# Attention on one core: pair 1 copied in two halves from two PSUM banks, and another set of VectorE groups

## Chip, cores and metric

The kernel runs on one core of a Trainium2 chip. The metric is device time in microseconds (us): the median of five runs. Times inside an execution come from the hardware profile of one run and count from its first instruction. The engines are TensorE (PE, with its weight loads as PEld), VectorE (DVE), ScalarE (ACT), GpSimd (POOL) and SyncE (SP), which issues most DMAs.

## The reference

Plain softmax attention for 8 x 8 = 64 heads, 512 queries and keys of 64 numbers each, fp32 in and out:

```python
batch, heads, seq, dim = 8, 8, 512, 64
scale = 1.0 / np.sqrt(q.shape[-1])
scores = np.einsum('bhqd,bhkd->bhqk', q, k) * scale
scores = scores - scores.max(axis=-1, keepdims=True)
attn = np.exp(scores)
attn = attn / attn.sum(axis=-1, keepdims=True)
return np.einsum('bhqk,bhkd->bhqd', attn, v).astype(np.float32)
```

## The kernel before

**Tiling.** The 64 heads are 32 pairs g of two heads h. For every head the 512 keys are four chunks c of 128. One block (g, c, h) is a score tile of 128 keys by 512 queries. Two blocks make a group m; there are 129 groups, the last two with one block each. Pair 0 has groups 0 to 3, pair 1 groups 4 to 7, and so on.

**The path of a pair.** The loads bring q, k, v in fp32 (`load`, L311). `cast` (L323) makes fp16 copies on GpSimd: q and k into `qkp`, v into `vp`, which also has a column of ones, so that the sum of the weights comes out of the value product. Only q of pair 1 is cast on VectorE. `transposes` (L377) runs four TensorE transposes for the keys and, at its second call, four for the queries, all into one PSUM tile `tp`. `copy` (L386) moves it to `tqk` in SBUF. `scores` (L398) multiplies a block of keys by the queries into a PSUM tile `st`, of which there are three; group m uses the one that group m - 3 used. ScalarE then takes the exponential of the group (L421) into `pt`.

**Eight groups on VectorE.** For the groups in `ON_DVE`, VectorE computes the exponential instead: `raise_` (L433) reads `st` into integers and frees it, and five passes (L448) finish it into `pd`. The passes can be done at any later time between other VectorE work.

**Values and output.** `values` (L495) is one unit of four matmuls into an `o` tile: 128 queries of one head. Seven units share a tile; the count of units begins at 4, so that the first tile holds three. `normalise` (L476) multiplies by the reciprocal of the sums into `ring`, from where the output is stored head by head.

**The two shared banks.** The tiles `tp` and `o` alternate in two PSUM banks, x0 and x1. A bank comes free when VectorE has copied or normalised what is in it.

**The order.** Every engine works through its instructions in program order, and that order is written by a planner, the class `Plan` (L17). It steps through time with assumed costs in nanoseconds (L31 to L38) and lets TensorE (`step_pe`, L168) and VectorE (`step_dve`, L191) choose their next piece of work. TensorE takes the next scores if their `st` tile is free and either the next group's is too, or the work that ScalarE has ahead of it (the backlog) is under `HURRY`, or the last thing was scores as well. If the tile is not free yet, but will be within `SOON` while the backlog is under `BACKLOG`, TensorE waits. Otherwise it takes transposes or value units. VectorE takes what is ready, a raise first; with nothing ready it starts a pass, unless a known copy would be late by more than `LATE_COPY` or a norm or raise by more than `LATE_NORM` at its end. A group is on VectorE by the list alone:

```python
    ON_DVE = (6, 15, 32, 44, 58, 69, 90, 103)

    LATE_NORM, LATE_COPY, HURRY, SOON, BACKLOG = 1000, 1400, 1000, 80, 1000
```

**Casts.** `feed(g)` (L364) is called with the first group of each pair. It loads pair g + 6 and casts later pairs; from pair 3 on the casts are held and given to GpSimd one at a time, each tied to the VectorE work before it (`release`, L348). `FIRST_VALUES` (L278) says which v is cast when in the first pairs. The first pair has its own opening, `first_pair` (L555), which leaves x0 and x1 to `tp_kb` and `tp_qb`; the planner takes over at group 3.

Of the kernel before, what the change touches and what calls it, by code (L numbers as in the profile page):

```python
# [9 lines left out]
FP16 = mybir.dt.float16  # L10
# [6 lines left out]
class Plan:  # L17
# [16 lines left out]
    TO_ACT, TO_DVE, TO_PE = 275, 210, 60  # L34

    COPY, NORM, RAISE = (615, 700), (307, 390), (1145, 1225)
    NORM_COLUMN, PASS_DONE = 67, 80
    PASSES = (650, 1230, 1230, 1230, 1230)  # L38
    FIRST_EXP = 5260
    STEP = 5  # L40
    FIRST_UNIT = 4
    ON_DVE = (6, 15, 32, 44, 58, 69, 90, 103)

    LATE_NORM, LATE_COPY, HURRY, SOON, BACKLOG = 1000, 1400, 1000, 80, 1000
    MARGIN, SLACK = 1.05, 0

    def __init__(self, groups, pairs, first):
# [37 lines left out]
    def for_dve(self, m):  # L85
        return m in self.ON_DVE

# [103 lines left out]
    def step_dve(self, t):  # L191
        now = [x for x in self.ready if x[0] <= t]
        if now:
            job = min(now, key=lambda x: (x[1] != "raise", x[0]))
            self.ready.remove(job)
            _, kind, what = job
            self.note(t, kind, *what)
            if kind == "norm":
                more = self.NORM_COLUMN * what[1]
                self.dve = t + self.NORM[0] + more  # L200
                self.banks[what[2]] = t + self.NORM[1] + more + self.TO_PE
            elif kind == "copy":
                self.dve = t + self.COPY[0]
                self.banks[what[1]] = self.tq[what[0]] = t + self.COPY[1] + self.TO_PE
            else:
                self.dve = t + self.RAISE[0]
                self.read[what[0]] = t + self.RAISE[1] + self.TO_PE
                self.passes += [(what[0], s) for s in range(len(self.PASSES))]
        elif self.passes:
            m, s = self.passes[0]  # L210
            end = t + int(self.MARGIN * self.PASSES[s])
            late = {"copy": self.LATE_COPY, "norm": self.LATE_NORM, "raise": self.LATE_NORM}
            if all(x[0] > end - late[x[1]] for x in self.ready):
                self.passes.pop(0)
                self.note(t, "pass", m, s)
                self.dve = end
                if s == len(self.PASSES) - 1:
                    self.exps[m] = end + self.PASS_DONE + self.TO_PE + self.SLACK
# [15 lines left out]
def kernel(  # L234
# [7 lines left out]
    nc = tc.nc  # L242
    B, H, S, D = q.shape
    P = 128
    NI = S // P
# [26 lines left out]
    ps_x = ctx.enter_context(tc.tile_pool(name="ps_x", bufs=1, space=bass.MemoryType.PSUM))  # L272
# [2 lines left out]

    HALVED = range(20, 25)
    AHEAD_FROM = 3
    FIRST_VALUES = {0: (), 1: (2,), 2: (1,), 3: (4,), 4: (5, 3), 5: (6, 7), 6: (8, 9)}  # L278
    NU = 56
    ring = cpool.tile([P, NU, D], FP32, name="ring")  # L280
    vps = [cpool.tile([P, 2, NI, D + 1], FP16, name=f"vp{n}") for n in range(NV)]
# [5 lines left out]
    tqk = {}  # L287
    tps = {}
# [51 lines left out]
    held = []  # L340
# [3 lines left out]
    def dve(ins):  # L344
        latest[:] = [ins]
        return ins

    def release(n=1):  # L348
        for g, name in held[:n]:
            ins = cast(g, name)  # L350
            if latest:
                tc.add_manual_dep(ins.ins, latest[0].ins.name, SYNC, reason="SBUF ports")
        del held[:n]

    def hold(g, names):
        held.extend((g, name) for name in names if g < NP)
        while len(held) > 6:
            cast(*held.pop(0))

    def needed(g, names):  # L360
        while any((g, name) in held for name in names):
            cast(*held.pop(0))

    def feed(g):  # L364
# [4 lines left out]
        if g >= AHEAD_FROM:  # L369
            hold(g + 4, "kq")  # L370
        for n in FIRST_VALUES.get(g, (g + 3,)):
            if g < AHEAD_FROM:
# [4 lines left out]
    def transposes(g, n, bank):  # L377
        if n == 0:
            needed(g, "kq")
            tqk[g] = tpool.tile([P, 2, S], FP16, tag="tqk", name=f"tqk_{g}")  # L380
            tps[g] = ps_x.tile([P, 2, NI, P], FP16, tag=f"x{bank}", name=f"tp_{g}")
        n = 1 - n
        for i in range(NI):
            nc.tensor.transpose(tps[g][:, n, i, :], qkp[g][:, n, i, :], ident)  # L384

    def copy(g):  # L386
        if g == 1:
            for n in (1, 0):
                dve(nc.vector.tensor_copy(out=tqk[g][:, n], in_=tps[g][:, n].rearrange("p i c -> p (i c)")))
            return  # L390
        release()
        dve(
            nc.vector.tensor_copy(  # L393
                out=tqk[g][:, :, :], in_=tps.pop(g).rearrange("p n i c -> p n (i c)")
            )
        )
# [247 lines left out]
    with tc.manual_schedule():  # L644
# [15 lines left out]
        for g, names in ((1, "kq"), (0, "v"), (2, "kq")):  # L660
            for name in names:
                cast(g, name)
        feed(0)
        do = {
            "transposes": transposes,
            "scores": scores,
            "values": values,
            "feed": feed,
            "raise": raise_,
            "copy": lambda g, b: copy(g),  # L670
            "pass": pass_,
            "norm": lambda u, n, b: normalise(u, n),
# [33 lines left out]
```

## Time and profile before

| | |
|---|---|
| five runs | 121.69, 122.01, 121.75, 122.77, 122.33 us; median 122.01 |
| the profiled execution | 122.12 us, of it a span of 120.3 us from first to last instruction |
| granted TensorE clock | 0.999 |
| busy in the span | ACT 112.6 us (94%), DVE 105.5 (88%), PE 103.0 (86%), POOL 66.6 (55%) |
| HBM traffic | read 25.17 MB, written 8.39 MB |
| exponentials on ScalarE (L421) | 118, 107.7 us busy |
| last exponential | ends at 116.5 us |

In the lines of a timeline the columns are start, length, engine, line of the program, operation, what is written and read, how often, and in brackets how long the engine stood idle before and which instruction ended that. Lines that merge several instructions give the time from the first start to the last end. Overlapping instructions of one engine, such as exponentials of which the next starts before the last has ended, count once in busy times.

### The profile page before, as it was taken

The numbers are of one execution on the slowest core, as the hardware profiler recorded it, in microseconds if no ns is written. First come the engines' busy times: TensorE is split into PE (matmuls) and PEld (weight loads), VectorE is DVE, ScalarE is ACT, GpSimd is POOL, SyncE is SP. The second block draws the span as 40 slices with busy tenths as digits, with TensorE's granted clock in tenths as the row PEclk, the third lists the DMA queues.
The fourth block names the chain that finished last, engine by engine and source line by source line (L and its number), as shares of the span: only waits on it lengthen the run. The fifth ranks groups of instructions, "written<-read, shape, count | busy, mean of one in ns | idle before, by whom it ended". The sixth has DMA issues, their size and how long they took to land.

```text
span 120.3 us, 4001 instructions
## 1 busy us (share of the span) xinstructions
PE 103.0 (86%) x1557; PEld 65.6 (55%) x1557; DVE 105.5 (88%) x177; ACT 112.6 (94%) x125; POOL 66.6 (55%) x101
## 2 busy tenths in 40 slices
PE   7969696988899789989897879999988989799970
PEld 2534353664656545845464548666655667367550
DVE  1549999999999999998999999999999999986261
ACT  4689998999999999999999999999999999999970
POOL 2358967999995656344958433596355654210000
PEclk9999999999999999999999999999999999999999
DMA  3999999999999999999999998999999812224243
GB/s 111 270 351 382 381 380 384 383 380 358 326 327 340 311 300 295 312 298 362 335 348 297 312 315 292 310 368 313 332 341 335 285 48 96 87 91 140 93 157 105
DMA packets 35604, 33.83 MB, mean 281 GB/s; under 512 B 2688, under 2 KB 35584, under 8 KB 35584
## 3 DMA queue, kind: packets, MB, share of 16 engines
q1 hardware_dynamic: 35152, 33.24, 83.9%
q10 hardware_dynamic: 432, 0.33, 0.9%
q8 instruction: 12, 0.20, 0.7%
q14 instruction: 8, 0.07, 0.2%
HBM read 25.17 MB, written 8.39 MB: 279 GB/s over the span
## 4 chain that ended last, share of the span: by engine, by line
DVE 29%; ACT 22%; DMA 17%; PE 17%; issue 8%; SPq 3%; POOL 1%; ACTq 0%; POOLq 0%
ACT pt L421 22%; DVE y L466 8%; PE st L416 8%; PE o L505 7%; DMA q<-in_q_dram 6%; DVE ring L482 6%; DVE tqk L393 5%; DMA out_dram<-ring 4%; DMA v<-in_v_dram 4%; DVE pd L466 3%; DVE z L438 3%; DVE m L454 2%; DMA k<-in_k_dram 2%; SPq L321 2%; PE tp L384 2%
## 5 line engine op out<-in xcount | busy, mean ns | idle before, releaser
L421 ACT ACTIVATE pt<-st 128x1024 f16<-128x1024 f32 (+1 forms) x118 | 107.7, 1204 | 1.2 <-PE st L416 1.2
L416 PE MATMUL st<-tqk 64*128 64x512 f16 x248 | 44.4, 382 | 6.6 <-ACT pt L421 5.3
L505 PE MATMUL o<-vp,pt 128*128 128x65 f16 x944 | 42.5, 194 | 2.7 <-DVE tqk L393 1.0
L505 PEld LDWEIGHTS <-pt 128*128 128x128 f16 x944 | 36.2, 98 | 14.7 <-issue 11.9
L333 POOL CAST qkp<-k 128x512 f16<-128x512 f32 x31 | 19.1, 615 | 23.7 <-PE st L416 5.6
L327 POOL CAST vp<-v 128x512 f16<-128x512 f32 x32 | 26.6, 836 | 4.9 <-DVE y L466 2.4
L333 POOL CAST qkp<-q 128x512 f16<-128x512 f32 x30 | 21.7, 725 | 7.7 <-DVE y L466 2.3
L482 DVE TENSOR_TENSOR ring<-o,rc 128x448 f32<-128x448 f32 (+2 forms) x37 | 22.6, 612 | 1.3
L416 PEld LDWEIGHTS <-tqk 64*128 64x128 f16 x248 | 12.2, 93 | 19.8 <-issue 13.1
L384 PE MATMUL tp<-ident,qkp 128*128 128x128 f16 x248 | 19.4, 220 | 3.1 <-DVE tqk L393 1.3
L466 DVE SCALAR_TENSOR_TENSOR y<-y,m 128x1024 f32<-128x1024 f32 x16 | 21.6, 1352 | 0.1
L384 PEld LDWEIGHTS <-qkp 128*128 128x128 f16 x248 | 14.3, 97 | 11.8 <-POOL qkp L333 5.6
L393 DVE COPY tqk<-tp 128x1024 f16<-128x1024 f16 x30 | 20.5, 682 | 0.0
L466 DVE SCALAR_TENSOR_TENSOR y<-m 128x1024 f32<-128x1024 uint32 x8 | 11.2, 1402 | 0.1
L480 DVE RECIPROCAL rc<-o 128x7 f32<-128x7 f32 (+2 forms) x37 | 7.2, 195 | 4.2 <-PE o L505 4.0
L438 DVE TENSOR_SCALAR z<-st 128x1024 uint32<-128x1024 f32 x8 | 9.7, 1217 | 0.7 <-PE st L416 0.7
L466 DVE SCALAR_TENSOR_TENSOR pd<-y,z 128x1024 uint32<-128x1024 f32 x8 | 10.3, 1283 | 0.0
L505 PE MATMUL o<-vp,pd 128*128 128x65 f16 x64 | 9.3, 194 | 0.0
L505 PEld LDWEIGHTS <-pd 128*128 128x128 f16 x64 | 6.3, 98 | 0.7 <-issue 0.5
L454 DVE TENSOR_SCALAR m<-z 128x1024 uint32<-128x1024 uint32 x8 | 6.3, 783 | 0.0
L553 PE MATMUL st_0a<-const-bfloat16-1.0 128*128 128x512 bf16 (+1 forms) x11 | 3.3, 457 | 0.8 <-PEq L690 0.8
L569 ACT ACT_TABLE_LOAD x1 | 1.3, 1283 | 1.7 <-PEq L690 1.7
(44 smaller groups left out, 18.8 us busy)
## 6 DMA issues: line engine op xcount, KB each, us to landing
out_dram<-ring SPq DMA_DIRECT2D x63, 128.0 KB, 3.9
k<-in_k_dram SPq DMA_DIRECT2D x31, 256.0 KB, 4.9
q<-in_q_dram SPq DMA_DIRECT2D x31, 256.0 KB, 5.0
v<-in_v_dram SPq DMA_DIRECT2D x27, 256.0 KB, 5.4
v<-in_v_dram SPq DMA_DIRECT2D x10, 128.0 KB, 3.8
k<-in_k_dram ACTq DMA_DIRECT2D x2, 128.0 KB, 2.7
q<-in_q_dram SPq DMA_DIRECT2D x2, 128.0 KB, 2.5
out_dram<-obl SPq DMA_DIRECT2D x1, 64.0 KB, 1.6
```

Of the source, the lines that this page charges most:

```text
L327: return nc.gpsimd.tensor_copy(out=vps[g % NV][:, :, :, 0:D], in_=raw[g]["v"][:, :, :, :])
L333: return eng.tensor_copy(out=qkp[g][:, "qk".index(name)].rearrange("p i (h d) -> p h i d", h=2), in_=raw[g][name][:, :, :, :],)
L384: nc.tensor.transpose(tps[g][:, n, i, :], qkp[g][:, n, i, :], ident)
L393: nc.vector.tensor_copy(out=tqk[g][:, :, :], in_=tps.pop(g).rearrange("p n i c -> p n (i c)"))
L416: nc.tensor.matmul(st[:, x, :], kc, qc, start=True, stop=True)
L421: nc.scalar.activation(out=pt[:, 0:size, :], in_=st[:, 0:size, :], func=EXP, scale=scale)
L438: nc.vector.tensor_scalar(out=r["z"][:, :, :], in0=r["st"][:, :, :], scalar1=scale * 1.4426950408889634 * 2.0**26, scalar2=15 * 2.0**26, o ...
L454: nc.vector.tensor_scalar(out=r["m"][:, :, :], in0=r["z"][:, :, :], scalar1=0x03FFFFFF, scalar2=0x04000000, op0=AluOp.bitwise_and, op1=Alu ...
L466: nc.vector.scalar_tensor_tensor(out=r["bits"][:, :, :] if n == 3 else r["y"][:, :, :], in0=r["m"][:, :, :] if n == 0 else r["y"][:, :, :] ...
L480: nc.vector.reciprocal(out=rc[:, 0:n], in_=o[:, x : x + n, D : D + 1])
L482: nc.vector.tensor_tensor(out=ring[:, u % NU : u % NU + n, :], in0=o[:, x : x + n, 0:D], in1=rc[:, 0:n].broadcast_to([P, n, D]), op=AluOp. ...
L505: nc.tensor.matmul(os[u // 7][:, u % 7, :], blocks[(g, c, h)][:, y * P : (y + 1) * P], vps[g % NV][:, h, c, :], start=(c == 0), stop=(c == ...
```

## The change

Three things are edited. First, pair 1: its keys and its queries are transposed into two PSUM tiles, the keys in the planner's bank and the queries in the other one (`bank ^ n`), and the copy of the keys is issued directly behind the keys' transposes; the planner's `copy` step then copies the queries alone. Second, the planner assumes other costs for that step, `COPY_1`. Third, the list of VectorE groups, four of the planner's limits and the order in which v of pairs 3 to 6 is cast are replaced.

```diff
     COPY, NORM, RAISE = (615, 700), (307, 390), (1145, 1225)
+    COPY_1 = (400, 490)
...
-    ON_DVE = (6, 15, 32, 44, 58, 69, 90, 103)
-
-    LATE_NORM, LATE_COPY, HURRY, SOON, BACKLOG = 1000, 1400, 1000, 80, 1000
+    ON_DVE = (6, 16, 34, 49, 61, 74, 87, 98)
+
+    LATE_NORM, LATE_COPY, HURRY, SOON, BACKLOG = 1300, 1400, 900, 220, 1600
...
             elif kind == "copy":
-                self.dve = t + self.COPY[0]
-                self.banks[what[1]] = self.tq[what[0]] = t + self.COPY[1] + self.TO_PE
+                held, done = self.COPY if what[0] != 1 else self.COPY_1
+                self.dve = t + held
+                self.banks[what[1]] = self.tq[what[0]] = t + done + self.TO_PE
...
-    FIRST_VALUES = {0: (), 1: (2,), 2: (1,), 3: (4,), 4: (5, 3), 5: (6, 7), 6: (8, 9)}
+    FIRST_VALUES = {0: (), 1: (2,), 2: (1,), 3: (3,), 4: (5, 6), 5: (4, 7), 6: (8, 9)}
...
             needed(g, "kq")
             tqk[g] = tpool.tile([P, 2, S], FP16, tag="tqk", name=f"tqk_{g}")
-            tps[g] = ps_x.tile([P, 2, NI, P], FP16, tag=f"x{bank}", name=f"tp_{g}")
+        if n == 0 or g == 1:
+
+            tps[g] = ps_x.tile([P, 2, NI, P], FP16, tag=f"x{bank ^ n}", name=f"tp_{g}_{n}")
         n = 1 - n
         for i in range(NI):
             nc.tensor.transpose(tps[g][:, n, i, :], qkp[g][:, n, i, :], ident)
-
-    def copy(g):
+        if g == 1 and n == 1:
+            copy(g, n)
+
+    def copy(g, n=0):
         if g == 1:
-            for n in (1, 0):
-                dve(nc.vector.tensor_copy(out=tqk[g][:, n], in_=tps[g][:, n].rearrange("p i c -> p (i c)")))
+            dve(
+                nc.vector.tensor_copy(
+                    out=tqk[g][:, n], in_=tps[g][:, n].rearrange("p i c -> p (i c)")
+                )
+            )
             return
```

## The prediction

> **What bounds the kernel now.** I read the page's busy shares first, then the windows by stage, then the timeline of ScalarE alone, then the timeline of every engine around pair 1 and of VectorE behind it. The windows show engine by engine how much of each stretch is filled.
>
> ```profile
> core 0: us, PE busy (x) PEld busy (x) DVE busy (x) ACT busy (x) POOL busy (x), PEclk, DMA share, GB/s
> 9.30:20.00 10.70, 8.19 (x110) 4.79 (x107) 10.44 (x13) 10.19 (x11) 8.69 (x11) 1.00 1.09 381
> ...
> 33.00:62.00 29.00, 26.24 (x408) 16.85 (x406) 28.18 (x44) 29.00 (x33) 17.96 (x29) 1.00 1.00 323
> 62.00:100.00 38.00, 34.30 (x542) 22.53 (x541) 37.38 (x56) 38.00 (x43) 20.93 (x34) 1.00 0.90 294
> ```
>
> From 33 to 100 us ScalarE (ACT) has work in every microsecond: 29.00 of 29.00, 38.00 of 38.00. VectorE is nearly as full (28.18, 37.38), but only its lateness can hurt, through what TensorE waits for. So the time is the run of exponentials plus the holes in it. ScalarE's own timeline shows the holes:
>
> ```profile
> 9.31 10.19 ACT L421 ACTIVATE pt<-st 128x1024 f16<-128x1024 f32 x11 [0.64 <-PE st L416]
> 20.04 96.50 ACT L421 ACTIVATE pt<-st 128x1024 f16<-128x1024 f32 x106 [0.54 <-PE st L416]
> ```
>
> Start, length, count; idle before in brackets. One exponential behind a hole takes 1.02 us; the ten others of the first stretch add (10.19 - 1.02) / 10 = 0.917 each. So each hole costs its idle plus 1.02 - 0.917 = 0.11 of lost overlap: 0.75 at the first group of pair 1 (m = 4) and 0.65 at m = 17. In the long stretch the last two half groups take 0.98, which leaves (96.50 - 0.98 - 1.02) / 103 = 0.9175, hence some 0.07 lost in 96 us. **All that can be won in the stream is 0.75 + 0.65 + 0.07 = 1.47 us.** The change keeps eight groups on VectorE, so the number of exponentials stays, and the 120.3 - 116.5 = 3.8 us behind the last exponential is untouched by its lines.
>
> **Pair 1's copies.** The timeline of all engines there:
>
> ```profile
> 7.02 0.43 DVE L333 CAST qkp<-q 128x512 f16<-128x512 f32 x1 [0.81 <-DMA q<-in_q_dram]
> ...
> 7.09 0.81 PE L384 MATMUL tp<-ident,qkp 128*128 128x128 f16 x8 [0.21 <-POOL qkp L333]
> 7.50 0.23 PEld L384 LDWEIGHTS <-qkp 128*128 128x128 f16 x4 [0.18 <-DVE qkp L333]
> ...
> 7.73 0.62 POOL L327 CAST vp<-v 128x512 f16<-128x512 f32 x1 [0.69 <-DMA v<-in_v_dram]
> 7.93 0.76 DVE L389 COPY tqk<-tp 128x512 f16<-128x512 f16 x2 [0.49 <-PE tp L384]
> 8.40 0.54 PE L505 MATMUL o<-vp,pt 128*128 128x65 f16 x12 [0.50 <-POOL vp L327]
> ...
> 8.87 0.82 PE L416 MATMUL st<-tqk 64*128 64x512 f16 x6
> ```
>
> The keys' four transposes are over before the queries' begin at 7.50, yet the keys' copy waits until 7.93, when all eight have ended. With the queries in the other bank it starts at about 7.52 and lasts 0.42 (the mean of these two); VectorE is free from 7.45. The queries' copy starts at 7.93 and ends at 8.36 instead of 8.69. Two copies, eight transposes, no DMA: no count changes. Bank x1, which the queries' tile now takes, was last read by the copy of tp_qb at 5.59 (0.42 long), so nothing waits for it. The first o tile takes the same bank and must now wait for the queries' copy, 8.36; its matmuls wait for the V cast until 8.35 anyway. That cover is 0.01 thin, and each ns past it would delay the first scores by as much.
>
> But what went ahead of the first scores at 8.87 was the twelve value matmuls, not the copy. Here the planner decides. I followed its rules by hand over pair 1 to 4 (its clock, in ns, is used for order alone). Before, the pair is due at 8745 and three value units go at 8300, 8430, 8560. Now it is due at 7985 + 490 + 60 = 8535; after one unit, at 8430, that is less than SOON = 220 off, so TensorE waits. Four matmuls instead of twelve: eight at a pitch of (0.54 - 0.19) / 11 = 0.032 are 0.25 us, so the scores start at 8.62 and the exponential at 9.05: **-0.25**. The bounds are nothing (V comes later) and -0.46 (scores right behind the copy, at 8.41).
>
> **What the new order does to VectorE behind it.** The two units left over hold bank x1; their normalisation moves behind raise 6 and copy 2. The planner puts scores 6 at 9885 instead of 9280 (the slot comes free 39 ns after the planner looks, with a backlog of 1885, over BACKLOG; a value unit, the transposes of pair 2 and another unit go first). So raise 6, the norm and the first two passes all precede copy 3. VectorE's timeline has the durations:
>
> ```profile
> 8.98 0.18 DVE L480 RECIPROCAL rc<-o 128x3 f32<-128x3 f32 x1 [0.29 <-PE o L505]
> 9.20 0.36 DVE L482 TENSOR_TENSOR ring<-o,rc 128x192 f32<-128x192 f32 x1
> 9.74 1.23 DVE L438 TENSOR_SCALAR z<-st 128x1024 uint32<-128x1024 f32 x1 [0.19 <-PE st L416]
> 10.88 0.68 DVE L393 COPY tqk<-tp 128x1024 f16<-128x1024 f16 x1
> 11.48 0.91 DVE L454 TENSOR_SCALAR m<-z 128x1024 uint32<-128x1024 uint32 x1
> 12.42 1.51 DVE L466 SCALAR_TENSOR_TENSOR y<-m 128x1024 f32<-128x1024 uint32 x1
> 13.85 0.68 DVE L393 COPY tqk<-tp 128x1024 f16<-128x1024 f16 x1
> ```
>
> Copy 2 can start at 10.2 (POOL's query cast for pair 2, on TensorE's path, ends at 9.14 + 0.62; four transposes 0.4), so raise 6 at 10.8. By starts: raise 1.14, norm 0.55, first pass 0.94, second 1.43, then the copy's 0.68: copy 3 ends at 15.54 instead of 14.53. Scores 12 take 0.39 and two hand-overs of 0.05: exponential 12 at 16.03. ScalarE would be ready earlier: from 9.05 seven exponentials (4, 5, 7 to 11) at 0.917 make the eighth end at 9.05 + 1.02 + 6.42 = 16.49, against 16.03 + 1.02 = 17.05. A **new hole of about 0.55**, where before there was none. If the passes ran at the 0.60 and 1.13 from start to start that they reach later in the trace (36 to 60 us), 0.64 less, it is nought.
>
> Next, by the same rules, passes three and four both go before copy 4 (17403 instead of 15360), and it sets scores 16 and 17. From 15.46 (VectorE free) come twice 1.51 and the copy's 0.68: 19.16; scores 16 and 17, 0.05 + 0.22 + 0.39 + 0.05: exponential 17 at 19.87, against 20.04. With as many exponentials ahead of it in both kernels, this one difference contains both steps above: **-0.17**. Bounds: with uncontended passes ScalarE alone decides, 9.05 + 1.02 + 11 x 0.917 = 20.16 for the end of m = 17 against 21.06 before, -0.90; with one more normalisation of seven columns (18.07 to 18.84, 0.77) ahead of copy 4, +0.60. I take -0.17: the windows show POOL busy 8.69 of 10.70 us there, so the contended rows are the nearest.
>
> [...]
>
> **The rest of the plan.** ON_DVE from 15 on, LATE_NORM, HURRY, SOON, BACKLOG: behind m = 17 the old choice loses 0.07, so there -0.07 is the whole possible gain. On the other side each new hole has the price of one seen here, 0.65. SOON and BACKLOG let TensorE wait for a score slot instead of starting value units; at 33 us the trace has such a case, three units in front of scores that wait. TensorE is idle for 10% of the two long stretches shown (26.24 of 29.00, 34.30 of 38.00), which pays for this. HURRY = 900 issues single scores later, LATE_NORM = 1300 lets VectorE finish a pass before a norm. I take **0 (between -0.07 and +2.0, three holes)**. The casts of V in another order (groups 3 to 5) cost nothing: the same 32 casts, each needed after a VectorE group or a pair has finished; one met late would cost its mean of 0.84. Eight groups over 92 steps instead of 97 leave VectorE full until about 106, as now (last pd at 105.76), so no wait there.
>
> **Sum.** -0.17 + 0 = -0.17 on 122.12 (the profiled execution: span 120.3 and 1.8 around it) is 121.95; it stands 0.11 over the median of 122.01, so 121.84: I say **121.8**.
>
> **Rivals.** (a) *Both holes close.* Passes run uncontended and only the rest of the first hole stays: 122.01 - 0.90 - 0.07 = 121.0. For it: the plan was given larger reserves for scores. Against: POOL's casts still sit beside passes one to four. (b) *Late norms, slower.* TensorE works in order; at m = 17 it stood 0.91 in front of transposes that waited for a ring write, with the scores behind them. LATE_NORM = 1300 allows VectorE 0.3 more of such lateness, and behind each of the six later VectorE groups two scores are due within one exponential. Two such holes: 122.01 - 0.17 + 2 x 0.65 = 123.1; every further one 0.65 more. It decides from 0.78 us of new holes, over 0.5% slower. Against it: over 96 us the old plan made almost none. (c) *Hidden anyway.* The scores come earlier, but copy 4 is delayed by a norm: 122.01 + 0.60 - 0.07 = 122.5.
>
> **How the numbers follow.** What tells from no change here is 0.5%, 0.61 us: below 121.40, above 122.62. Forecast 0.42 (own range 121.0 to 122.5), (a) 0.22, (b) 0.22, (c) 0.14. Faster: all of (a) and a quarter of the forecast, 0.33. Slower: (b) and a fifth of (c), 0.25. Same: 0.42. The range runs from 120.7 (the full 1.47 gained is 120.5) to 123.1.
>
> **What would show it.** Scores of pair 1 behind four value matmuls at 8.6 and an exponential at 9.05; copy 3 near 15.5 with a hole before m = 12; m = 17 near 19.9; ScalarE full from there to about 116.4. The prediction is wrong if ScalarE idles over 0.6 us behind 21 us, or if copy 3 ends before 15.

## The result

| | before | after |
|---|---|---|
| median of all runs beside each other | 122.11 us (121.07 to 124.21, 94 runs) | 122.51 us (121.84 to 125.18, 54 runs) |
| ratio | 1 | 1.004 (95% interval 1.0029 to 1.0052) |
| the profiled execution | 122.12 us, span 120.3 | 122.67 us, span 120.9 |

The changed kernel is 0.4% slower, by the ratio 0.49 us (0.35 to 0.63); the medians are 0.40 us apart. The forecast was 0.17 us faster. A few executions of several kernels, the one before among them, took 130 to 450 us and are left out everywhere, those of the profiles of `e2` and `e17` included, and the ratio also leaves out runs over 1.5% above the fastest of their kernel (nine and six of this table).

**Profile after, the stream of exponentials.** ScalarE's timeline of the changed kernel (start, length, what, count, idle before and its releaser):

```profile
8.19 19.02 ACT L430 ACTIVATE pt<-st 128x1024 f16<-128x1024 f32 x20
27.62 89.08 ACT L430 ACTIVATE pt<-st 128x1024 f16<-128x1024 f32 x98 [0.41 <-PE st L425]
```

The two holes of before, at m = 4 and m = 17, no longer split the line: they are down to 0.19 and 0.21 us, counted as before against a pitch of 0.917. But a small one has come at m = 12 (0.19) and a new one at m = 25, 27.62 us (0.51 with its lost overlap). Together 1.09 instead of 1.47. Still the last exponential ends at 27.62 + 89.08 = 116.70, where before it ended at 116.54. What was won in holes is lost ahead of them: the first exponential of the opening begins at 5.14 here and at 4.83 in the profile before, and a hole of 0.24 stands at m = 2.

**The end.** All engines' timelines, last lines, first of before and then of after (the last store's issue):

```profile
117.60 0.33 SPq L540 DMA_DIRECT2D out_dram<-obl  x1
117.60 0.37 ACTq L540 DMA_DIRECT2D out_dram<-obl  x1
```

```profile
117.76 0.33 SPq L549 DMA_DIRECT2D out_dram<-obl  x1
117.77 0.37 ACTq L549 DMA_DIRECT2D out_dram<-obl  x1
```

The store goes out 1.06 us behind the last exponential in both. From there to the end of the span it is 120.26 - 117.60 = 2.66 us before and 120.89 - 117.76 = 3.13 after (3.72 and 4.19 counted from the last exponential; with the repeats of both kernels below 3.73 and 4.18 in the mean, 0.45 apart). No line of the kernel is busy in this difference. What differs is GpSimd's closing drain, 220 ns instead of 78, which begins 0.33 later behind the last exponential (3.55 instead of 3.22), and the queues on the page; before, then after (packets, MB, share of 16 engines):

```profile
q14 instruction: 8, 0.07, 0.2%
```

```profile
q14 instruction: 7, 0.06, 0.2%
```

One of the 8 KB instruction transfers of queue q14 has gone from the inside of the span to behind it: before, the last two are at 108.42 and 110.72 us, after at 110.82 and 121.19. This last one begins 0.30 us behind the end of the span, when the longer drain is over, so it is a sign that goes with the longer end and not the thing waited for. GpSimd's traced instructions went from 204 to 201.

**TensorE between 12.7 and 19.5 us.** Windows of before and then of after (busy time of each engine, granted clock, DMA share, GB/s):

```profile
core 0: us, PE busy (x) PEld busy (x) DVE busy (x) ACT busy (x) POOL busy (x), PEclk, DMA share, GB/s
12.70:16.10 3.40, 2.16 (x20) 1.03 (x18) 3.40 (x4) 3.40 (x5) 3.40 (x4) 1.00 1.09 379
16.10:19.50 3.40, 2.43 (x46) 1.80 (x44) 3.37 (x5) 3.39 (x4) 2.16 (x4) 1.00 1.09 383
```

```profile
12.70:16.10 3.40, 1.73 (x24) 0.96 (x24) 3.37 (x4) 3.32 (x5) 2.64 (x4) 1.00 1.10 387
16.10:19.50 3.40, 1.69 (x24) 0.97 (x23) 3.33 (x5) 3.40 (x4) 2.67 (x3) 1.00 1.08 375
```

TensorE is busy for 50% of these 6.8 us instead of 68%, since it now waits 1.67 and 1.71 us for copies 3 and 4. In this profile the clock stays full there. In others it does not: the mean granted clock of an execution was 0.9865 or less in 22 of the changed kernel's 78 runs (this table's and its two repeats'), whose median is 123.59 us; the other 56 have 122.43. The limit parts two groups: no run of any kernel lies between 0.986 and 0.988, and a stretch of 3.41 us at a clock of 0.50, as the profile of `e9` further on shows it, takes 0.014 off the mean of 120.9 us. The kernel before never was below it in the 152 runs beside the experiments; the clocks of its 94 runs in the table are not on record, and nine of these took over 123 us. Against the median of the kernel before beside them, the changed kernel's runs with a full clock are 0.33 us slower in the table (39 runs) and -0.10 and 0.29 in the repeats (10 and 7), 0.25 in the weighted mean.

### The profile page after: what moved, and what is told of

Same layout as the page of the kernel before. It is cut to its first block, busy times and chain, and to the rows that moved or that the text cites. A ratio compares the mean times of both kernels' runs of the same rounds, so it can differ in the third digit from the quotient of the medians.

```text
span 120.9 us, 3996 instructions
## 1 busy us (share of the span) xinstructions
PE 103.2 (85%) x1557; PEld 65.8 (54%) x1557; DVE 105.0 (87%) x177; ACT 112.9 (93%) x125; POOL 66.0 (55%) x101
## 4 chain that ended last, share of the span: by engine, by line
DVE 35%; ACT 28%; PE 22%; issue 9%; DMA 2%; SPq 0%; ACTq 0%
ACT pt L430 28%; DVE y L475 10%; PE st L425 9%; DVE ring L491 7%; DVE tqk L402 5%; DVE z L447 5%; PE o L514 5%; PE tp L388 3%; DVE pd L475 3%; PE st_0a L562 3%; DMA out_dram<-ring 2%; DVE rc L489 2%; DVE m L463 2%; PE st L605 1%; DVE tqk L395 1%
## 5 line engine op out<-in xcount | busy, mean ns | idle before, releaser
L335 POOL CAST qkp<-k 128x512 f16<-128x512 f32 x31 | 21.8, 705 | 18.6 <-DVE rc L489 4.8
L329 POOL CAST vp<-v 128x512 f16<-128x512 f32 x32 | 24.0, 756 | 11.5 <-DVE y L475 9.2
L425 PEld LDWEIGHTS <-tqk 64*128 64x128 f16 x248 | 12.8, 93 | 23.9 <-issue 12.4
L335 POOL CAST qkp<-q 128x512 f16<-128x512 f32 x30 | 20.4, 681 | 7.9 <-DVE y L475 3.5
L475 DVE SCALAR_TENSOR_TENSOR y<-y,m 128x1024 f32<-128x1024 f32 x16 | 21.1, 1321 | 0.0
L475 DVE SCALAR_TENSOR_TENSOR pd<-y,z 128x1024 uint32<-128x1024 f32 x8 | 11.0, 1369 | 0.1
L475 DVE SCALAR_TENSOR_TENSOR y<-m 128x1024 f32<-128x1024 uint32 x8 | 9.9, 1242 | 0.1
L562 PEld LDWEIGHTS <-const-bfloat16-1.0 128*128 128x128 bf16 x15 | 1.7, 131 | 2.4 <-issue 2.4
```

The costliest lines, as they stand in the source:

```text
L329: return nc.gpsimd.tensor_copy(out=vps[g % NV][:, :, :, 0:D], in_=raw[g]["v"][:, :, :, :])
L335: return eng.tensor_copy(out=qkp[g][:, "qk".index(name)].rearrange("p i (h d) -> p h i d", h=2), in_=raw[g][name][:, :, :, :],)
L425: nc.tensor.matmul(st[:, x, :], kc, qc, start=True, stop=True)
L475: nc.vector.scalar_tensor_tensor(out=r["bits"][:, :, :] if n == 3 else r["y"][:, :, :], in0=r["m"][:, :, :] if n == 0 else r["y"][:, :, :] ...
```

## The experiments

Three suspicions came out of this: the end (0.45 us), the clock (22 of 78 runs by 1.16 us, 0.33 in the mean), and new holes. Ratios are to the kernel before, run on the same chip in the same rounds. "Low clock" is a run with a mean granted clock of 0.9865 or less.

### Both kernels again

`e0` is the kernel before, `e1` and, on another chip, `e8` the changed one, no edit.

> The kernel before, unchanged, as the yardstick for one profile against another. Theory O (the opening of the changed kernel's profile was late by chance: full TensorE clock granted at 5.83 us instead of 3.92, first exponential at 5.14 instead of 4.83): the opening of an unchanged kernel varies too, between about 4.8 and 5.2 for the first exponential. Theory C (the lateness belongs to the changed code): full clock near 3.9 and first exponential near 4.83 again. Both: holes of 0.75 at m = 4 and 0.65 at m = 17 again, ratio 1.00.

> The changed kernel, unchanged, for a second profile. Theory O: the opening may come out either way, and with an opening at 4.83 the hole at m = 4 grows from 0.19 towards the 0.49 that was forecast; ratio 1.004. Theory C: full clock near 5.8 us and first exponential near 5.14 again. Both expect the hole of about 0.5 at m = 25 and about 0.2 each at m = 12 and 17, if these belong to the order of work.

> The changed kernel again, as the yardstick for the next three on one chip: holes of about 0.2 at m = 4, 12 and 17, 0.3 to 0.6 at m = 25, 4.15 to 4.18 us from the last exponential to the end, ratio 1.000 to 1.006.

Measured: `e0` 0.9995 (0.9974 to 1.0016), `e1` 0.9998 (0.9972 to 1.0024) with 2 of 12 runs at low clock, `e8` 1.0055 (1.0028 to 1.0082) with 5 of 12. So one set of 12 runs can hide the whole effect. The profile of `e0` taught more than its time. All engines around pair 1:

```profile
7.48 0.62 PE L384 MATMUL tp<-ident,qkp 128*128 128x128 f16 x8
...
7.94 0.54 PE L505 MATMUL o<-vp,pt 128*128 128x65 f16 x12
8.14 0.76 DVE L389 COPY tqk<-tp 128x512 f16<-128x512 f16 x2 [0.92 <-PE tp L384]
8.29 2.10 ACT L421 ACTIVATE pt<-st 128x1024 f16<-128x1024 f32 x2
...
8.95 0.82 PE L416 MATMUL st<-tqk 64*128 64x512 f16 x6 [0.47 <-DVE tqk L389]
```

This is the kernel before, and its hole at m = 4 is 0.17, not 0.75: exponential 3 follows its predecessor without a break and ends at 9.31, 0.65 later than in the profile that the prediction read. And the twelve value matmuls are out of the way at 8.48, in the shade of the copies, which end at 8.90; scores follow at 8.95. Two things differ between the two executions. TensorE gets its full clock at 3.92 us in the profile before and at 6.08 in `e0`, at 5.83 in the changed kernel's profile and at 5.13 in that of `e15`. And V, which the value matmuls need, is cast by 7.70 us in `e0` and by 8.35 in the profile before, where its load landed later. Which of the two weighs more is not shown.

### The split alone, the plan alone

`e2` is the kernel before with the split and the changed code, but with the old groups, limits, cast order and cost; `e3` is the changed kernel with one pair of copies as before, at the old cost.

```diff
 e2, against before: the change's edits of transposes and copy, and
+    COPY_1 = (615, 700)
 e3, against after: those edits undone, groups, limits and FIRST_VALUES kept
-    COPY_1 = (400, 490)
```

> Pair 1 in two tiles, with the groups, limits, costs and order of the kernel before. Theory A (what went ahead of the first scores of pair 1 was the twelve value matmuls, not the copy; the split gains nothing without a new order): the exponential of m = 4 at 9.3 with a hole of 0.75 as before, ratio 0.998 to 1.002. Rival (the copy sets the scores): scores 0.3 us earlier, hole 0.45, ratio 0.997. If the split itself does harm (an added wait on the other bank), ratio 1.004.

> The new groups, limits and order of V casts, with pair 1 copied as before at the old planned cost. Theory P (the new plan costs the time: limits let TensorE start long runs of value units in front of scores, as at m = 25): slower, ratio 1.004 to 1.010, with holes behind 21 us of over 0.5 in sum. Rival (the plan is neutral, the loss is the split's): ratio 0.998 to 1.002.

Measured: `e2` 1.0008 (0.999 to 1.0027), no low clock in its 11 usable runs; `e3` 1.0102 (1.0066 to 1.0137), low clock in 4 of 6. ScalarE's timeline of `e3`:

```profile
8.28 11.27 ACT L421 ACTIVATE pt<-st 128x1024 f16<-128x1024 f32 x12
19.86 2.85 ACT L421 ACTIVATE pt<-st 128x1024 f16<-128x1024 f32 x3 [0.31 <-PE st L416]
23.61 37.69 ACT L421 ACTIVATE pt<-st 128x1024 f16<-128x1024 f32 x41 [0.90 <-PE st L416]
61.62 56.08 ACT L421 ACTIVATE pt<-st 128x1024 f16<-128x1024 f32 x62 [0.32 <-PE st L416]
```

The split by itself brings nothing that can be measured (what became of its hole at m = 4 was not seen). The new groups without it cost 1%, by holes at 23.61 (1.01) and 61.62 (0.43) and by the low clock; the two runs with a full clock are 0.78 us over the kernel before. The limits and groups belong to the new cost: the planner's order hangs on every number. And `e3` ends 3.73 us behind its last exponential, with 204 traced instructions on GpSimd as before: the longer end does not come with the plan as such.

### The end, taken away and made

`e4` gives GpSimd four more instructions behind everything, `e5` gives the kernel before three fewer; `e9` is `e4` once more, on the chip and in the rounds of `e8`.

```diff
 e4, e9, against after, behind the planner's loop
+        scratch = cpool.tile([P, 4], FP16, name="scratch")
+        for n in range(4):
+            nc.gpsimd.memset(scratch[:, n : n + 1], 0.0)
 e5, against before, in release
-            if latest:
+            if latest and g < 31:
```

> The changed kernel with four more GpSimd instructions, tiny memsets of an unused tile behind its last cast, where GpSimd is idle. Theory F (the changed kernel's GpSimd program is three waits shorter, 201 instead of 204 traced instructions, so that its next block of code is crossed into only inside the closing sequence, where nothing hides it): four more instructions bring the crossing ahead of the last barrier again; from the last exponential to the end 3.74 us instead of 4.18, GpSimd's closing drain 78 ns instead of 206 to 220, no code transfer behind 120 us, stream of exponentials as in the changed kernel; ratio 0.996 to 1.000. Rival (the longer end belongs to the work, say the last stores): 4.18 stays, ratio 1.000 to 1.004.

> The kernel before with three GpSimd waits fewer: the casts of pair 31 alone are no longer tied to the VectorE work ahead of them. Theory F: from the last exponential to the end about 4.18 us instead of 3.74, ratio 1.003 to 1.004, all else as before. Rival (the longer end belongs to the changed order of work): 3.74 and ratio 1.000.

> The changed kernel with four more GpSimd instructions, a second time: 3.72 us behind the last exponential; by theory F its median is 0.2 to 0.6 us under that of the changed kernel on the same chip. If it is not, the 0.43 us seen in the profiles does not reach the time.

Measured, from the last exponential to the end of the span: `e4` 3.72, `e5` 4.15 with the drain at 220 ns and one q14 transfer at 121.63, behind the end. Page and last store, first of `e4` and then of `e5`:

```profile
span 120.8 us, 4000 instructions
118.17 0.33 SPq L549 DMA_DIRECT2D out_dram<-obl  x1
```

```profile
span 121.3 us, 3998 instructions
118.21 0.33 SPq L540 DMA_DIRECT2D out_dram<-obl  x1
```

So a few instructions of GpSimd switch the longer end on and off, in either kernel. All usable profiles agree: with 201 traced GpSimd instructions the end is 4.15 to 4.20 us (five profiles), with 204 or 205 it is 3.71 to 3.77 (thirteen). The times followed in `e5`, 1.0029 (1.0005 to 1.0053, one of 12 runs at low clock), but not clearly in `e4`, 1.0023 (0.9995 to 1.0051), nor in `e9`, 1.0022 (0.9996 to 1.0049), whose median of 122.92 lies over the 122.72 of `e8`. Its five runs at low clock do that: without them and without the five of `e8` it is 122.38 against 122.65. Another likely reason came out later (`e16`): the padding itself slowed the loads.

### The holes

`e6` moves scores 25 ahead of the value units that hold them up; `e7` also puts copies 3 and 4 ahead of the passes; `e10` puts scores 4 and 5 ahead of the first value unit; `e11` does all of it; `e15` is `e11` again on another chip. All carry the padding of `e4`. The whole edit, of which each takes its part:

```diff
+        ahead(("feed", 1), ("values", 0, 0, 0, 4, 1))             # e10, e11
+        ahead(("scores", 4, False), ("values", 0, 0, 0, 4, 1))    # e10, e11
+        ahead(("scores", 5, False), ("values", 0, 0, 0, 4, 1))    # e10, e11
+        ahead(("scores", 25, False), ("values", 3, 0, 0, 28, 1))  # e6, e7, e11
+        ahead(("copy", 3, 1), ("pass", 6, 1))                     # e7, e11
+        ahead(("copy", 4, 1), ("pass", 6, 3))                     # e7, e11
```

`ahead` takes the first step out of the planned list and puts it in front of the second.

> As with the four more GpSimd instructions, and the scores of m = 25 moved ahead of the seven value units that stood in front of them. Theory H (the hole before m = 25, 0.27 to 0.51, is made by value units run ahead of due scores, as HURRY = 900 lets the planner): that hole is gone, no other takes its place, stream 0.3 shorter, ratio 0.993 to 0.997. Rival (m = 25 waits for its score tile, the order does not matter): hole of 0.3 to 0.5 stays.

> As the one before, and on VectorE copy 3 moved ahead of the second pass of group 6 and copy 4 ahead of its fourth pass. Theory D (the holes before m = 12 and m = 17, 0.2 each, come from these copies standing behind passes): both gone, the sum of holes 0.2 to 0.4 instead of 0.8 to 1.1, ratio 0.990 to 0.995. Rival (the later raise of group 16 or another norm takes over): a new hole of 0.2 or more between m = 18 and 24.

> Four more GpSimd instructions, and the scores of m = 4 and 5 moved ahead of the one value unit in front of them. Theory V (that unit needs bank x1, which the queries' copy now frees only at 8.57, and V, and so it stands between the copy and the scores): scores of pair 1 within 0.1 us behind the end of the queries' copy instead of 0.3, hole at m = 4 under 0.1 with a late full clock and under 0.4 with an early one. Rival (the scores wait for the copy alone): no difference, hole 0.17 to 0.19.

> All moves together: four more GpSimd instructions, scores of m = 4 and 5 ahead of the value unit, copies 3 and 4 ahead of a pass each, scores of m = 25 ahead of seven value units. Sum of holes 0.8 to 1.3, ratio 0.992 to 0.998 and below that of the changed kernel by 0.5 us or more. If moves of single steps only shift the holes, ratio 1.000.

> All moves together a second time (GpSimd, scores of m = 4 and 5, copies 3 and 4, scores of m = 25): ratio 0.995 to 1.000. If the first result of 0.9976 was chance, 1.000 to 1.004.

| | ratio | interval | low clock |
|---|---|---|---|
| `e6` | 0.9995 | 0.9964 to 1.0027 | 5 of 12 |
| `e7` | 0.9977 | 0.9956 to 0.9997 | 3 of 12 |
| `e10` | 1.0009 | 0.9983 to 1.0035 | 3 of 12 |
| `e11` | 0.9976 | 0.9951 to 1.0001 | 3 of 11 |
| `e15` | 1.0016 | 0.9991 to 1.004 | 0 of 12 |

The holes at m = 12, 17 and 25 go when what stands in front of them is moved. TensorE's timeline of the changed kernel shows the cause of the one at m = 25:

```profile
24.67 0.61 PE L425 MATMUL st<-tqk 64*128 64x512 f16 x4
25.43 0.61 PE L388 MATMUL tp<-ident,qkp 128*128 128x128 f16 x8 [0.15 <-DVE rc L489]
26.20 1.05 PE L514 MATMUL o<-vp,pt 128*128 128x65 f16 x28 [0.16 <-POOL qkp L335]
27.19 0.82 PE L425 MATMUL st<-tqk 64*128 64x512 f16 x6
```

Seven value units, 28 matmuls or 1.05 us, stand in front of the scores that ScalarE waits for at 27.6. In `e6` that hole is gone (though small ones of 0.10 to 0.14 come at m = 28, 35 and 38), and in `e7` those at 12 and 17, though the clock falls at 19.07 us there and a hole of 0.54 follows at 21. The one at m = 4 is another matter: in `e10` the scores begin 0.06 us behind the end of the queries' copy (9.48 against 9.42), as theory V has it, but the hole is 1.10 instead of under 0.4, since the transposes waited until 8.00 for the cast of the keys, whose load had landed late. The best is the profile of `e11`, ScalarE's timeline:

```profile
8.42 107.98 ACT L430 ACTIVATE pt<-st 128x1024 f16<-128x1024 f32 x118
```

All 118 in one line, 0.56 us of holes in all, the last ending at 116.40. But `e15`, the same kernel, had holes of 2.12 us and ended its last exponential at 117.66: its full clock came at 5.13 us, and its transposes of pair 1 waited until 7.96 for a cast on GpSimd. A single profile is no measure of the holes in the opening. The times are less clear than the holes: of the ranges expected for `e6`, `e7` and `e11` only that of `e11` was met, and the 1.0016 of `e15` is what its expectation calls chance.

### The clock

`e12` fills TensorE's two waits for the copies with ten dummy matmuls into the score tile that is written next; `e13` has the padding of `e4` too. `e14` is the kernel before, with copies 3 and 4 put one pass later, so that TensorE is idle longer there; in its profile it waits 2.57 us for copy 3 and not at all for copy 4.

```diff
 e12, e13, against after, in scores
+        for n in range({12: 6, 16: 4}.get(m, 0)):
+            busy(st[:, 0], S)
 e14, against before
+        ahead(("pass", 6, 2), ("copy", 3, 0))
+        ahead(("pass", 6, 3), ("copy", 4, 0))
```

> The changed kernel with ten more matmuls of 512 columns that nothing reads, six in front of the scores of m = 12 and four in front of those of m = 16, into the score tile that the scores then overwrite: TensorE waits there for 1.67 and 1.71 us anyway. Theory K (idle TensorE loses its full clock for 3.41 us in some runs): no run of 12 with a mean clock between 0.970 and 0.987 and none over 123.1 us; holes and the end as in the changed kernel (4.15 to 4.18), ratio 1.000 to 1.003. Rival (the low clock has another cause): about 3 or 4 of 12 runs as slow as before, and slower by what the matmuls delay.

> The same ten matmuls and the four more GpSimd instructions. Theories K and F together: no low clock, 3.72 us behind the last exponential, ratio 0.996 to 1.000, and 0.2 to 0.6 us under the run with the matmuls alone. If the longer end does not reach the time, no difference between the two.

> The kernel before with copies 3 and 4 each moved behind one more VectorE pass, so that TensorE waits for them about 1.5 us longer each. Theory K: mean clocks of 0.970 to 0.987 in 2 to 8 of 12 runs, where the kernel before has none; ratio 1.005 to 1.015 with the added holes. Rival: slower by the holes alone, no low clock.

Measured: no low clock in the 24 runs of `e12` and `e13`, low clock in 3 of 6 of `e14` (123.83 to 124.13 us against 122.48 to 122.7 for the other three). In `e12` TensorE is busy for 89% of the 6.8 us, instead of 50%:

```profile
12.70:16.10 3.40, 3.11 (x29) 1.56 (x29) 3.37 (x4) 3.35 (x5) 2.61 (x4) 1.00 1.10 387
16.10:19.50 3.40, 2.93 (x30) 1.46 (x28) 3.33 (x5) 3.40 (x4) 2.52 (x3) 1.00 1.07 375
```

So in these runs longer idle time of TensorE brought the low clock, and filling the idle time took it away. `e15`, beside them and without the filling, had none in 12 runs either; but `e16` (below), which is filled too and ran on the chip where `e8` and `e9` had 5 of 12 each, had none in 11. The waits for copies 3 and 4 are not the only ones that can do it: with these copies moved ahead, 3 of 12 runs of `e7` and 3 of 11 of `e11` were still low. What a drop looks like, in the windows of `e9`'s profile:

```profile
16.64:20.04 3.40, 1.70 (x23) 0.81 (x20) 3.33 (x6) 3.30 (x5) 1.75 (x3) 1.00 1.08 344
20.04:23.45 3.41, 3.41 (x31) 1.93 (x29) 2.91 (x3) 3.15 (x4) 2.31 (x4) 0.50 1.09 348
23.45:26.85 3.40, 3.39 (x67) 2.29 (x65) 3.31 (x7) 3.06 (x4) 3.40 (x6) 1.00 1.09 362
```

A stretch with TensorE busy for half of it, then 3.41 us at a clock of 0.50 in which it is busy all through with 31 matmuls, then 67 matmuls in the next 3.40: it has to catch up, and ScalarE has gaps meanwhile (3.15 and 3.06 busy). So half idle was enough, but in a part of the runs only. Which part is open: counted in steps of 3.41 us from the moment of the full clock, TensorE is busy for 50 to 52% of two steps in a row in the profiles of the changed kernel, `e1`, `e4` and `e6`, and the clock stays; in `e9` and `e10` it falls behind two steps of 50 to 56%, and in `e7` behind one of 62% (2.10 of 3.41 us). By the ratio, `e12` is at 1.0023 (1.0002 to 1.0045): about half of the loss is left, with a full clock and with an end of 4.20 us in its profile. `e13`, with the end of 3.75, is no better: 1.0026 (1.0002 to 1.005).

### The end without a side effect

Why did the padding not pay? Windows of the first 20 us, first of `e12`, then `e13`, last of `e16` (GB/s at the end of the line):

```profile
0.00:20.00 20.00, 17.45 (x154) 9.44 (x155) 12.98 (x36) 16.56 (x20) 12.38 (x23) 1.00 0.95 323
```

```profile
0.00:20.00 20.00, 16.73 (x149) 8.53 (x151) 13.01 (x36) 16.36 (x20) 10.91 (x21) 1.00 0.96 303
```

```profile
0.00:20.00 20.00, 17.01 (x154) 8.49 (x155) 13.24 (x36) 16.66 (x20) 12.20 (x22) 1.00 0.94 320
```

The padded kernel moves 303 GB/s instead of 323, with its DMA engines no less busy (0.96). So it is in all profiles: 296 to 308 GB/s in the eight with this padding, 317 to 325 in the other ten, and apart on each of the three chips that had both. All eight have the scratch tile of 8 bytes a partition, whose pool stands ahead of that of the loads. That it shifts the tiles that the loads write, and so slows them, was the author's guess; the record has no addresses, so that is not shown. `e16` is `e13` with a scratch tile of 1024 bytes, of which the same four columns are set; `e17` is `e11` with it.

```diff
-        scratch = cpool.tile([P, 4], FP16, name="scratch")
+        scratch = cpool.tile([P, 512], FP16, name="scratch")
```

> [...] Theory (the 0.43 us of the longer end is real, and the first padding hid it by slowing the loads): some 6.1 MB landed by 20 us instead of 5.8, 3.72 us from the last exponential to the end, no execution with the low clock, ratio 0.997 to 1.000, 0.2 to 0.6 us below the relation of the kernel with the dummy matmuls alone (1.0023). Rival (the longer end is of the profiled executions only): the end is as short and the ratio is 1.001 to 1.004 all the same.

> [...] Theory: the holes before exponentials 4, 12, 17 and 25 are gone or under 0.2 us, the loads are as fast as in the changed kernel and the end is 3.72 us; ratio 0.990 to 0.997, below both kernels. [...]

Measured: `e16` 0.999 (0.9974 to 1.0007), `e17` 0.9935 (0.9915 to 0.9956), median 121.56 against 122.30. The loads of `e16` run at 320 GB/s again (the megabytes of the expectation leave out 0.33 MB of queue q10). Its end, page and timeline:

```profile
span 120.0 us, 4019 instructions
```

```profile
117.36 0.33 SPq L551 DMA_DIRECT2D out_dram<-obl  x1
117.37 0.37 ACTq L551 DMA_DIRECT2D out_dram<-obl  x1
```

That is 2.66 us behind the store, as before (120.02 - 117.36). Beside `e12`, which differs in the padding alone, it is 0.0033 or 0.40 us lower; beside `e13`, which differs in the width of the scratch tile alone, 0.44 us. Each of these differences is uncertain by some 0.003, from the two intervals together, and is taken between two chips; `e11` and `e15`, one kernel on the same two chips, differ by 0.0040. So it is likely, and not shown, that the end is worth about its 0.45 us in the time too. No usable run of either was at low clock; with five usable runs of `e17`, and 3 of 11 low in `e11`, that says little about `e17`. `e17` is faster than both kernels by more than its interval, though the changed one did not run beside it. That its holes are the few of `e11` rests on `e11`'s profile.

## Why the prediction was wrong

**The sum.** With both unforeseen costs out of the way, the change measures near what the sum said: `e16`, the changed kernel with a full clock and the old end, stands at 0.999, -0.12 us (-0.32 to +0.09), against -0.17 forecast; no change lies in that interval too. That is partly luck, since single terms were off in both directions, as said below. What the sum lacked is +0.45 at the end and the low clock. None of the prediction's own signs of being wrong came: behind 21 us ScalarE idled for 0.41 us, not over 0.6, and copy 3 did not end before 15. They watched the stream of exponentials, and the loss lay outside it.

**Where it failed.** The step is "the 120.3 - 116.5 = 3.8 us behind the last exponential is untouched by its lines". No line of the diff stands there, and yet it grew by 0.45, because the number of GpSimd's instructions changed ahead of it (`e4`, `e5`, `e16`). That the fetch of one more code block is what GpSimd waits for was a guess from the q14 transfer that moved; the number of instructions is shown as the cause, the fetch is not, and why the drain begins later and takes longer stays open.

The second gap is in the step from copy 3 at 15.54 to exponential 17. It priced TensorE's longer wait for copies 3 and 4 by what ScalarE loses (0.55 and a net -0.17), not by what TensorE's idling does to its own clock: 1.16 us more in 28% of the runs, in the mean 0.33. That cost stood at nothing in the sum.

**Pair 1 at 8.62 and 9.05, -0.25.** The order was right: one value unit, then scores. The start was 8.86 instead of 8.62, since the cover "0.01 thin" gave way: all engines around pair 1 in the changed kernel,

```profile
7.38 0.62 PE L388 MATMUL tp<-ident,qkp 128*128 128x128 f16 x8
...
7.61 0.62 POOL L329 CAST vp<-v 128x512 f16<-128x512 f32 x1 [0.75 <-DMA v<-in_v_dram]
7.81 0.76 DVE L395 COPY tqk<-tp 128x512 f16<-128x512 f16 x2 [0.49 <-PE tp L388]
8.19 2.12 ACT L430 ACTIVATE pt<-st 128x1024 f16<-128x1024 f32 x2
...
8.63 0.30 PE L514 MATMUL o<-vp,pt 128*128 128x65 f16 x4 [0.63 <-DVE tqk L395]
8.86 0.61 PE L425 MATMUL st<-tqk 64*128 64x512 f16 x4
```

V is cast at 8.23, but the value unit stands still until the queries' copy frees its bank at 8.57, and the scores behind it wait with it. In `e0` the copies end 1.42 us behind the start of the transposes and the scores begin 1.47 behind it; here 1.19 and 1.48. The split wins 0.23 on the copies and gives it back to the bank. In `e11`, with the scores first, they begin 1.25 behind the transposes. And the hole that this step was to shrink was mostly that one profile's: 0.75 there, 0.17 in `e0`, where the twelve value matmuls were done before the copies ended, so that it was the copies and not the matmuls that the scores waited for.

**Copy 3 at 15.54, the hole of 0.55, m = 17 at 19.87, -0.17.** Very near, as VectorE's timeline after shows:

```profile
12.40 1.15 DVE L463 TENSOR_SCALAR m<-z 128x1024 uint32<-128x1024 uint32 x1
13.58 1.22 DVE L475 SCALAR_TENSOR_TENSOR y<-m 128x1024 f32<-128x1024 uint32 x1
14.72 0.68 DVE L402 COPY tqk<-tp 128x1024 f16<-128x1024 f16 x1
15.32 3.14 DVE L475 SCALAR_TENSOR_TENSOR y<-y,m 128x1024 f32<-128x1024 f32 x2
18.39 0.68 DVE L402 COPY tqk<-tp 128x1024 f16<-128x1024 f16 x1
```

Copy 3 ended at 15.40, in the order foreseen; passes three and four took 1.53 each from start to start, where 1.51 was taken. Exponential 17 began at 19.77 here (19.92 and 19.99 in the repeats). The hole was 0.19 and not 0.55, because the exponentials ahead came later. The -0.17 itself was measured against 20.04, the start in one profile; `e0` has 19.88, so that -0.07 is left of it over the means. Which of a pass and a cast beside it takes longer differs: here the second pass ran 1.14 from start to start and not the row's 1.43, while the cast that began inside it, at 13.76, took 1.52 us, and the one at 12.38 took 0.62; in the profile before, passes three and four, each begun 0.10 behind the start of a cast, took 1.51, and those two casts 0.61. The first pass took 1.18, not 0.94; the two errors cancelled by chance (2.32 against 2.37), and the sum came out by the rows all the same.

**The rest of the plan, 0.** Behind m = 17 the changed kernel lost 0.51 (0.27 and 0.26 in the repeats) at m = 25 and nothing else: one hole at about half the assumed price, where the sum had 0, by value units in front of scores and not by late norms.

**The rivals.** (a) took 121.0: not reached by the change, though `e17` with the moves comes to 121.56. (b) was right in sign, but not in its place or cause: the loss is at the end and in the clock. (c) with 122.5 has the right number by another road; its norm ahead of copy 4 went behind it, at 18.99.

**What stays open.** The three parts don't add up: end (+0.45), clock (+0.33 in the mean) and last exponential (116.66 over three profiles after, 116.61 over two before) make 0.83, while the means of all runs of the table are 0.53 apart (122.74 and 122.20). The runs with a full clock show it best: 0.25 in the weighted mean, where the end alone asks for 0.45. Either the stream of a usual run has gained some 0.2, more than the few profiles show, or the profiled runs are not typical ones, or the end costs less in the time than in the profiles.

## To carry to other kernels

A wait that costs the busiest engine nothing may still cost TensorE its clock (here 1.16 us in 28% of the runs): look at TensorE's busy share over stretches as long as the drop in `e9`, 3.41 us, and at the granted clock of all runs instead of the profiled one. The first microseconds of a profile vary with the moment of the full clock (3.92 to 6.08 us in the four profiles named) and with the landing of the first loads, so a hole found there should be seen in a second profile before a change is priced by it. And when something is added only to test a thought, see whether it changes anything else: with the tile of 8 bytes the first 20 us moved 303 GB/s (`e13`), without it 323 (`e12`).

## What the runs showed of the hardware

- **Half idle can be enough.** With TensorE busy for 50% of 6.8 us (the profile after) the mean granted clock of an execution was 0.9865 or less in 28% of the runs, with 68% (the profile before) in none of 152; in the profile of `e9` the drop was to 0.50 for 3.41 us. A safe share is not known from this: with 67% of these 6.8 us in the profile of `e3`, 4 of its 6 runs were low.
- **A few instructions at the end.** Three fewer on GpSimd lengthened the end, counted from the last exponential, from 3.73 to 4.15 us (`e5`, against the kernel before), four more shortened it from 4.18 to 3.72 (`e4`, against the changed kernel), with the closing drain at 206 to 220 ns in the longer ends instead of 78; an 8 KB instruction transfer behind the end went with the longer one (121.19 us in the changed kernel, 121.63 in `e5`).
- **A small tile and the loads.** With a scratch tile of 8 bytes a partition the first 20 us moved 296 to 308 GB/s instead of 317 to 325, with one of 1024 bytes 320 (`e16`), and between `e13` and `e16`, which differ in this width alone, lie 0.44 us (two chips). Why the narrow tile goes with slower loads is not shown.
